# The opening of a fused attention layer: loads issued by three engines, forget columns loaded apart, squares shared, and the small weights cast on GpSimd

## The chip, the cores and the metric

The kernel runs on one core of a Trainium2 chip, as one launch. The metric is the device time of a launch in microseconds (us), lower is better. A core has five engines, each with its own in-order instruction queue: TensorE (PE in the profile, its weight loads PEld), VectorE (DVE), ScalarE (ACT), GpSimd (POOL) and SyncE (SP). 16 DMA engines serve them all.

## The reference

One layer over 512 rows of x behind 16 learned meta rows (L = 528), width 1024, all in float32:

```python
u = rmsnorm(h, pre_norm_g)
proj = u @ w_in
(cq, ckv, k_pe_raw, z_mla, fq, fk, fv, f_logit, z_fox, gate_a, gate_b) = split(proj)
q  = rmsnorm(cq, g_q) @ w_uq;  kv = rmsnorm(ckv, g_kv) @ w_ukv
y_mla = (attention(q, kv, rope(k_pe_raw)) * silu(z_mla)) @ w_br_mla
cum = cumsum(log_sigmoid(f_logit + fox_forget_b))
y_fox = (attention(fq, fk, fv, cum) * silu(z_fox)) @ w_br_fox
out = h + rmsnorm((sigmoid(gate_a) * y_mla + sigmoid(gate_b) * y_fox) @ w_out, g_post)
```

The opening, which the change touches, computes u and the four narrow pieces of proj: cq (256 columns of w_in), ckv (128), k_pe_raw (32), which lie side by side, and f_logit (16 columns, "forget columns"), which lie far off at column 4512.

## The kernel before

Each float32 product is made of three TensorE products in a narrower format: an operand is split into a high half (h) and a low half (l), and h*h, l*h and h*l are summed in PSUM. Splitting takes a cast (the high half) and a subtraction (the low half), and these are what ScalarE, VectorE and GpSimd do for most of the kernel.

The opening works on five blocks of rows: t = 0 to 3 are 128 rows of x each, t = 4 is the 16 meta rows. For each block:

- `load_h(t)` loads it into `ht`; block 0 comes as two halves of 512 columns, both issued by SyncE.
- `squares(t)` sums the squares of each row on ScalarE (tile `hn` takes the squares, `st` the sums), then square root and reciprocal. For block 0 the halves are two ScalarE instructions.
- `scaled(t)` multiplies the rows on VectorE (tile `hn`).
- `turn(t)` transposes it on TensorE in eight pieces of 128x128, into `pt`.
- `turned(t, 0, ..)` writes the high half of u transposed, `uTh`, on ScalarE, and `turned(t, 1, ..)` the low half, `uTl`, on VectorE, eight instructions each. `turned_all(4)` does it for the meta rows.
- `small(t, which, ks)` multiplies it with the narrow weights, into the PSUM tile `psm`: per k (eight pieces of 128 rows of the weights) the products 0 (uTh, wsh), 1 (uTl, wsh) and 2 (uTh, wsl).
- `back(t)` and `latent(t)` normalise the results (`sm`) and transpose them (`pc`).

The narrow weights, 432 columns, come in four quarters c (two k each), raw in `wsr`: for every quarter one load of 416 columns (128 partitions x 2 x 1664 B) and one of the 16 forget columns (128 x 2 x 64 B). `small_hi(c)` casts quarter c into `wsh`: quarters 0, 2 and 3 on ScalarE, quarter 1 on GpSimd. `small_lo(c)` subtracts into `wsl`: quarters 0 and 1 on GpSimd, 2 and 3 on VectorE. `spun` is a product whose result nobody reads: ten of them (512 columns) run on TensorE while the first loads are under way, and four more behind `turn(0)`. `wsplit` (wh, wl) splits all later weights in the same way, wh on ScalarE and wl on GpSimd.

The order in which the code calls these sets the order of TensorE's queue (`manual_schedule`). On the other engines a planner orders the instructions, but those wrapped in `pin` (`keep_in_program_order`) stay in the order of the code; `free` leaves the planner a choice. SyncE's loads share eight semaphores in turn, so a ninth load is issued once the first has landed.

Ahead of all this VectorE clears CT and ONE, and GpSimd makes the identity matrix `ident` for the transposes and clears KPL and `fa`. Behind it come the first projections (fq, fk, ppe, v) and 16 attention stages, then the branch products, gates and the output.

## Time and profile before

| | |
|---|---|
| three runs | 604.13, 604.9, 605.65 us, median 604.9 |
| profiled execution | 603.71 us, its span 601.8 us (1.9 us around it) |
| TensorE busy | 592.5 us, 98% of the span |
| VectorE, ScalarE, GpSimd busy | 374.1, 343.9, 180.6 us |
| granted TensorE clock | 0.998 |
| DMA moved | 93.25 MB, 155 GB/s on average |

The span runs from the first to the last instruction of the program. A row of the timeline has the start, the length, the engine, the line, the operation, the tiles out<-in and their shapes, and in brackets how long the engine sat idle before it and who ended that. "DMA a<-b" is a transfer. Rows of several instructions carry their count (x8), and their length is that of the whole group. Line numbers are those of the kernel before.

### The profile page before, as it was taken

How to read it: one execution, taken by the hardware profiler on the slowest of the kernel's cores; microseconds unless marked ns; L12 is line 12 of the kernel's file. 1: busy time of each engine (PE TensorE's matmuls, PEld its weight loads, DVE VectorE, ACT ScalarE, POOL GpSimd, SP SyncE). 2: the span in 40 equal slices, each digit the busy share in tenths (PEclk: the TensorE clock that was granted, in tenths of full speed). 3: DMA queues.
4: the chain of work that ended last, by engine and by line, in shares of the span. 5: the costliest groups of instructions: out<-in, count | busy, mean ns of one | idle time of the engine just before them, and what ended most of it. 6: DMA issues, size and time to landing. Idle time of an engine off the chain costs nothing.

```text
span 601.8 us, 10999 instructions
## 1 busy us (share of the span) xinstructions
PE 592.5 (98%) x3777; PEld 501.7 (83%) x3777; DVE 374.1 (62%) x1002; ACT 343.9 (57%) x788; POOL 180.6 (30%) x239
## 2 busy tenths in 40 slices
PE   8999999999999999999999999999999999999996
PEld 6889779789889889888898898888888888888884
DVE  4956776674675674766657747764733524367857
ACT  7847765774783784766747747851222423353653
POOL 4316635443348453443523534430000000000000
PEclk9999999999999999999999999999999999999999
DMA  8433699899796798988886875988533333332603
GB/s 294 107 84 86 134 196 208 193 189 231 96 185 152 171 200 178 189 191 170 163 158 154 201 160 140 193 163 281 182 97 105 106 86 89 105 104 91 228 0 141
DMA packets 219960, 93.25 MB, mean 155 GB/s; under 512 B 133420, under 2 KB 211636, under 8 KB 219904
## 3 DMA queue, kind: packets, MB, share of 16 engines
q1 hardware_dynamic: 219904, 92.55, 65.5%
q8 instruction: 30, 0.49, 0.3%
q14 instruction: 26, 0.21, 0.1%
HBM read 58.10 MB, written 4.00 MB: 103 GB/s over the span
## 4 chain that ended last, share of the span: by engine, by line
PE 92%; ACT 3%; DMA 2%; DVE 1%; issue 1%; POOL 1%; SPq 0%; DVEq 0%; ACTq 0%; POOLq 0%
PE z L97 16%; PE py L97 14%; PE pg L97 14%; PE v L97 9%; PE st L97 8%; PE fq L97 8%; PE fk L97 7%; PE ov L97 5%; PE x L97 4%; PE psm L97 2%; PE mq L97 2%; PE mk L97 1%; PE ppe L97 1%; DMA wsr<-in_w_in_dram 1%; PE y L97 1%; DMA ht<-in_x_dram 1%
## 5 line engine op out<-in xcount | busy, mean ns | idle before, releaser
L103 POOL TENSOR_TENSOR wl<-wraw,wh 128x1024 fp32r<-128x1024 f32 (+2 forms) x63 | 122.6, 1954 | 105.3 <-ACT wh L130 76.5
L130 ACT CAST wh<-wraw 128x1024 fp32r<-128x1024 f32 (+1 forms) x80 | 83.1, 1042 | 115.7 <-PE pg L97 38.6
L823 DVE SCALAR_TENSOR_TENSOR pn<-sf,ri,pn 128x128 f16<-128x128 f32 (+3 forms) x128 | 70.7, 592 | 13.9 <-ACT pn L822 13.8
L795 ACT ACTIVATE sf<-sf,nb 128x144 f32<-128x144 f32 (+3 forms) x128 | 72.0, 564 | 8.1 <-DVE nb L787 7.8
L822 ACT ACTIVATE pn<-sf,ri 128x128 f16<-128x128 f32 (+3 forms) x128 | 61.5, 551 | 20.4 <-ACT sf L795 17.6
L103 DVE TENSOR_TENSOR wl<-wraw,wh 128x1024 fp32r<-128x1024 f32 x33 | 40.3, 1223 | 42.4 <-ACT wh L130 42.4
L787 DVE CUSTOM_DVE_ANT_0 sf<-st,maskt 128x272 f32<-128x272 f32 (+2 forms) x128 | 48.6, 435 | 3.9 <-PE st L97 3.9
L97 PE MATMUL z<-uTh,wh 128*128 128x512 f32 x128 | 50.9, 398 | 0.0
L97 PE MATMUL z<-uTh,wl 128*128 128x512 f32 x128 | 50.1, 392 | 0.3 <-POOL wl L103 0.3
L97 PE MATMUL pg<-uTh,wh 128*128 128x512 f32 x128 | 50.3, 393 | 0.0
L97 PE MATMUL z<-uTl,wh 128*128 128x512 f32 x128 | 50.0, 391 | 0.0
L97 PE MATMUL pg<-uTl,wh 128*128 128x512 f32 x128 | 49.8, 389 | 0.0
L97 PE MATMUL pg<-uTh,wl 128*128 128x512 f32 x128 | 49.8, 389 | 0.0
L97 PE MATMUL py<-gh,wh 128*128 128x512 f32 x128 | 49.8, 389 | 0.0
L97 PE MATMUL py<-gl,wh 128*128 128x512 f32 x128 | 49.8, 389 | 0.0
L97 PE MATMUL py<-gh,wl 128*128 128x512 f32 x128 | 49.8, 389 | 0.0
L97 PE MATMUL st<-hlk,hlq 64*128 64x272 f32 (+3 forms) x480 | 47.3, 306 | 0.0
L97 PEld LDWEIGHTS st<-hlk,hlq 64*128 64x128 f32 x480 | 35.0, 185 | 5.8 <-ACT vh L719 2.8
L700 DVE TENSOR_REDUCE vsc<-v 128x1 f32<-128x272 f32 (+1 forms) x32 | 13.2, 432 | 37.9 <-PE v L97 37.9
L97 PE MATMUL v<-uTh,wl 128*128 128x256 f32 (+1 forms) x128 | 36.5, 285 | 0.0
L97 PE MATMUL fk<-uTl,wh 128*128 128x256 f32 (+1 forms) x128 | 36.4, 285 | 0.0
L97 PE MATMUL fk<-uTh,wh 128*128 128x256 f32 (+1 forms) x128 | 36.4, 285 | 0.0
(233 smaller groups left out, 1431.4 us busy)
## 6 DMA issues: line engine op xcount, KB each, us to landing
wraw<-in_w_in_dram SPq DMA_DIRECT2D x56, 512.0 KB, 4.1
wraw<-in_w_br_fox_dram SPq DMA_DIRECT2D x8, 512.0 KB, 3.6
tb<-in_w_out_dram SPq DMA_DIRECT2D x8, 512.0 KB, 7.4
wraw<-in_w_br_mla_dram SPq DMA_DIRECT2D x8, 512.0 KB, 3.6
wraw<-in_w_out_dram SPq DMA_DIRECT2D x6, 512.0 KB
pt<-pn SPq DMA_TRANSPOSE x128, 3.1
xr<-in_x_dram SPq DMA_DIRECT2D x4, 512.0 KB, 7.4
out_dram<-yo SPq DMA_DIRECT2D x8, 256.0 KB, 2.0
```

Of the source, the lines that this page charges most:

```text
L97: nc.tensor.matmul(*a, **k)
L103: return eng.tensor_tensor(out=lo, in0=src, in1=f32(hi), op=ALU.subtract)
L130: nc.scalar.copy(wh[:, :n], raw[:, :n])
L700: nc.vector.tensor_reduce(out=sc[:, i : i + 1], in_=ps, op=ALU.max, axis=AX.X, apply_absolute_value=True)
L787: nc.vector.tensor_tensor_reduce(out=sf_of(h, b)[:, c0 : c0 + w], in0=ps[h][:, o : o + w], in1=maskt[:, m0 : m0 + w], scale=-scale, scalar ...
L795: exps[g] = nc.scalar.activation(sf, sf, AF.Exp, bias=sums["nb"][:, h, b : b + 1], scale=-1.0, accum_out=sums["su"][:, h, b : b + 1]).ins
L822: nc.scalar.activation(hi, sf, AF.Copy, scale=rib)
L823: nc.vector.scalar_tensor_tensor(out=lo, in0=sf, scalar=rib, in1=hi, op0=ALU.mult, op1=ALU.subtract)
```

## The change

Six edits, all in the opening:

1. The second half of block 0 is issued by ScalarE, ahead of its table load and its first square root (`warm`), which now follow it.
2. The forget columns of all four quarters come in one load of their own (tile `wf`, 128 x 8 x 64 B), issued by GpSimd; `wsr` keeps 416 columns. GpSimd clears KPL behind that.
3. Block 0's second half is squared on VectorE (`tensor_tensor_reduce`), the first on ScalarE.
4. GpSimd casts the forget columns and all four quarters; it subtracts the forget columns, then quarters 0 and 1 as before.
5. TensorE runs the products of k = 0, 1 of block 0 ahead of `turn(1)`.
6. Eight and three `spun` instead of ten and four.

```diff
--- before.py
+++ after.py
@@ -234,7 +234,6 @@
     nc.vector.memset(f32(ONE), 0.0)
     for h in range(2):
         nc.vector.memset(f32(ONE[64 * h : 64 * h + 2, :]), 1.0)
-    nc.gpsimd.memset(f32(KP[1]), 0.0)
     hls = {}
 
     def hl_done(key, n, w):
@@ -276,7 +275,7 @@
         ppt = ph.enter_context(tc.tile_pool(name="ppt", bufs=2, space=PSUM))
         pps = ph.enter_context(tc.tile_pool(name="pps", bufs=2, space=PSUM, side="right"))
         warm = pa1.tile([1, 16], F32, tag="warm", name="warm")
-        nc.scalar.activation(warm[:, 0:1], eps_t[0:1, 0:1], AF.Sqrt)
+        pin = tc.keep_in_program_order
 
         hts = {}
         halves = (slice(0, 512), slice(512, D))
@@ -286,14 +285,18 @@
             pool, tag = (wp, "wraw") if t < 3 else (pa, "ht")
             hts[t] = pool.tile([128, D], F32, tag=tag, name=f"ht{t}")
             if t == 0:
-                for sl in halves:
-                    nc.sync.dma_start(hts[t][:, sl], x2[0:128, sl])
+                nc.sync.dma_start(hts[t][:, halves[0]], x2[0:128, halves[0]])
+                pin(nc.scalar.dma_start(hts[t][:, halves[1]], x2[0:128, halves[1]]))
             elif t < 4:
                 nc.sync.dma_start(hts[t], x2[128 * t : 128 * t + 128])
             else:
                 nc.sync.dma_start(hts[t][0:META], meta_tokens)
 
         load_h(0)
+        pin(nc.scalar.activation(warm[:, 0:1], eps_t[0:1, 0:1], AF.Sqrt))
+        wf = pa1.tile([128, KD, NH], F32, tag="wf", name="wf")
+        nc.gpsimd.dma_start(wf, win[:, :, O_F : O_F + NH])
+        nc.gpsimd.memset(f32(KP[1]), 0.0)
 
         g8 = pa1.tile([KD, 128], F32, tag="g8", name="g8")
         nc.sync.dma_start(g8, pre_norm_g[0].rearrange("(k p) -> k p", p=128))
@@ -304,17 +307,16 @@
         wsr = []
         nsm0 = NSM - NH
         for c in range(4):
-            r = pa.tile([128, 2, NSM], F32, tag="wsr", name=f"wsr{c}", bufs=4)
-            nc.sync.dma_start(r[:, :, 0:nsm0], win[:, 2 * c : 2 * c + 2, 0:nsm0])
-            nc.sync.dma_start(r[:, :, nsm0:], win[:, 2 * c : 2 * c + 2, O_F : O_F + NH])
+            r = pa.tile([128, 2, nsm0], F32, tag="wsr", name=f"wsr{c}", bufs=4)
+            nc.sync.dma_start(r, win[:, 2 * c : 2 * c + 2, 0:nsm0])
             wsr.append(r)
 
         def small_hi(c, copy):
-            return copy(wsh[:, 2 * c : 2 * c + 2, :], wsr[c])
+            return copy(wsh[:, 2 * c : 2 * c + 2, 0:nsm0], wsr[c])
 
         def small_lo(c, eng):
             cs = slice(2 * c, 2 * c + 2)
-            return eng.tensor_tensor(out=wsl[:, cs, :], in0=wsr[c], in1=f32(wsh[:, cs, :]), op=ALU.subtract)
+            return eng.tensor_tensor(out=wsl[:, cs, 0:nsm0], in0=wsr[c], in1=f32(wsh[:, cs, 0:nsm0]), op=ALU.subtract)
         for t in (2, 4, 3):
             load_h(t)
         gq = pa1.tile([128, R_Q + R_KV], F32, tag="gq", name="gq")
@@ -342,8 +344,9 @@
             st1 = sts[t] = pa.tile([128, 16], F32, tag="st1", name=f"st1_{t}")
             if t == 0:
 
-                for i, sl in enumerate(halves):
-                    pin(nc.scalar.activation(hn[:, sl], ht[:, sl], AF.Square, accum_out=st1[:, 2 + i : 3 + i]))
+                pin(nc.scalar.activation(hn[:, halves[0]], ht[:, halves[0]], AF.Square, accum_out=st1[:, 2:3]))
+                pin(nc.vector.tensor_tensor_reduce(out=hn[:, halves[1]], in0=ht[:, halves[1]], in1=ht[:, halves[1]], scale=1.0,
+                                                   scalar=0.0, op0=ALU.mult, op1=ALU.add, accum_out=st1[:, 3:4]))
                 pin(nc.vector.tensor_scalar(out=st1[:, 0:1], in0=st1[:, 2:3], scalar1=1.0 / D, scalar2=EPS, op0=ALU.mult,
                                             op1=ALU.add))
                 pin(nc.scalar.activation(st1[:, 1:2], st1[:, 3:4], AF.Sqrt, bias=st1[:, 0:1], scale=1.0 / D))
@@ -450,10 +453,9 @@
 
         order = tc.manual_schedule(engines={mybir.EngineType.PE})
         ph.enter_context(order)
-        pin = tc.keep_in_program_order
         free = lambda ins: ins
         spun = acc("spun")
-        for _ in range(10):
+        for _ in range(8):
             mm(spun, ONE, CT[:, 0:512], start=True, stop=True)
         gps = ppt.tile([128, 4, 128], F32, tag="pt", name="gps")
         tps(gps[:, 0, 0:KD], g8, ident[0:KD, 0:KD])
@@ -461,22 +463,23 @@
         scaled(0, pin)
         pin(nc.vector.tensor_copy(gcol, gps[:, 0, 0:KD]))
         turn(0)
-        for _ in range(4):
+        for _ in range(3):
             mm(spun, ONE, CT[:, 0:512], start=True, stop=True)
         squares(1, pin)
         scaled(1, pin)
-        pin(small_hi(0, nc.scalar.copy))
-        turn(1)
-        pin(small_hi(1, nc.gpsimd.tensor_copy))
+        pin(nc.gpsimd.tensor_copy(wsh[:, :, nsm0:], wf))
+        for c in range(4):
+            pin(small_hi(c, nc.gpsimd.tensor_copy))
         turned(0, 0, range(KD), pin)
         turned(0, 1, range(KD), pin)
-        for c in (2, 3):
-            pin(small_hi(c, nc.scalar.copy))
+        small(0, (0, 1), range(2))
+        turn(1)
+        pin(nc.gpsimd.tensor_tensor(out=wsl[:, :, nsm0:], in0=wf, in1=f32(wsh[:, :, nsm0:]), op=ALU.subtract))
         for c in (0, 1):
             pin(small_lo(c, nc.gpsimd))
         turned(1, 0, range(KD), pin)
         turned(1, 1, range(KD), pin)
-        small(0, (0, 1))
+        small(0, (0, 1), range(2, KD))
         small(1, (0, 1))
         for c in (2, 3):
             pin(small_lo(c, nc.vector))
```

On TensorE, from the first transposes on (pt out of hn are transposes of a block, psm are products with the narrow weights), before:

```order
L100 MATMUL pt_1_190<-ident,hn_175 128x128 x4
L97 MATMUL spun<-CT,ONE 128x512 x4
L100 MATMUL pt_0_206<-ident,hn_199 128x128 x4
L100 MATMUL pt_1_211<-ident,hn_199 128x128 x4
L97 MATMUL psm_253<-wsh,uTh 128x432
L97 MATMUL psm_253<-wsh,uTl 128x432
```

and of the change:

```order
L100 MATMUL pt_1_186<-ident,hn_171 128x128 x4
L97 MATMUL spun<-CT,ONE 128x512 x3
L97 MATMUL psm_221<-wsh,uTh 128x432
L97 MATMUL psm_221<-wsh,uTl 128x432
L97 MATMUL psm_221<-wsh,uTh 128x432
L97 MATMUL psm_221<-wsh,uTl 128x432
L100 MATMUL pt_0_226<-ident,hn_194 128x128 x4
L100 MATMUL pt_1_231<-ident,hn_194 128x128 x4
L97 MATMUL psm_221<-wsh,uTh 128x432
```

Four products of block 0 moved ahead of the transposes of block 1 (hn_199 before, hn_194 now). The rest of TensorE's queue is the same.

On GpSimd, from its first use of the narrow weights to the subtraction of the first later weights (wl), before:

```order
L328 MEMSET fa 16x528
L313 COPY wsh<-wsr_135 128x864
L317 TENSOR_TENSOR wsl<-wsr_132,wsh 128x864
L317 TENSOR_TENSOR wsl<-wsr_135,wsh 128x864
L103 TENSOR_TENSOR wl_582<-wraw_579,wh_581 128x1024
```

and of the change, with its load:

```order
L298 DMA wf<-in_w_in_dram 128x8x16
masks.py:199 ISA
masks.py:199 AFFINE_SELECT ident<-ident 128x128
L299 MEMSET KPL 128x528
L330 MEMSET fa 16x528
L470 COPY wsh<-wf 128x8x16
L315 COPY wsh<-wsr_134 128x2x416
L315 COPY wsh<-wsr_136 128x2x416
L315 COPY wsh<-wsr_138 128x2x416
L315 COPY wsh<-wsr_140 128x2x416
L477 TENSOR_TENSOR wsl<-wf,wsh 128x8x16
L319 TENSOR_TENSOR wsl<-wsr_134,wsh 128x2x416
```

One cast became five, and they stand ahead of the two subtractions; ScalarE has none of them any more.

On VectorE, between the subtractions of quarters 2 and 3 and the results of block 0 (st_2, st_4, st_3 and hn are the scaling of blocks 2, 4 and 3; um and uTl<-um the meta rows; tm and sm belong to back(0)), before:

```order
L317 TENSOR_TENSOR wsl<-wsr_141,wsh 128x864
L333 RECIPROCAL st_2_290<-st_2_290 128x1
L358 TENSOR_SCALAR hn_289<-ht_144,st_2_290 128x1024
L333 RECIPROCAL st_4_296<-st_4_296 16x1
L358 TENSOR_SCALAR hn_295<-ht_146,st_4_296 16x1024
L390 TENSOR_TENSOR um_0_358<-pt_0_340,gcol 128x64
L390 TENSOR_TENSOR um_1_362<-pt_1_345,gcol 128x64
L423 TENSOR_TENSOR tm_319<-psm_253,rt 128x16
L333 RECIPROCAL st_3_302<-st_3_302 128x1
```

and of the change:

```order
L319 TENSOR_TENSOR wsl<-wsr_140,wsh 128x2x416
L335 RECIPROCAL st_2_287<-st_2_287 128x1
L361 TENSOR_SCALAR hn_286<-ht_142,st_2_287 128x1024
L335 RECIPROCAL st_4_293<-st_4_293 16x1
L361 TENSOR_SCALAR hn_292<-ht_144,st_4_293 16x1024
L335 RECIPROCAL st_3_299<-st_3_299 128x1
L361 TENSOR_SCALAR hn_298<-ht_146,st_3_299 128x1024
L426 TENSOR_TENSOR tm_316<-psm_221,rt 128x16 x4
L335 RECIPROCAL st_0_313<-st_0_313 128x2
L393 TENSOR_TENSOR um_0_355<-pt_0_337,gcol 128x64
L428 TENSOR_TENSOR sm_312<-tm_316 128x32
```

The planner put the scaling of block 3 and most of back(0) ahead of the meta rows. On ScalarE the square of block 3 stands ahead of the first square of back(0) now, not behind it.

## The prediction

> **What bounds the kernel now.** I read the shares by engine first, then the chain that ended last over the first 62 us, then the timeline of each engine over the first 34 us.
>
> ```profile
> PE 592.5 (98%) x3777; PEld 501.7 (83%) x3777; DVE 374.1 (62%) x1002; ACT 343.9 (57%) x788; POOL 180.6 (30%) x239
> ```
>
> TensorE (PE) is busy for 98% of the span, so only a stage in which it waits can give time back. The chain of waits, whose columns are start, length and what held the end, shows where that is:
>
> ```profile
> 2.05 4.12 DMA ht<-in_x_dram
> 6.19 5.47 DMA wsr<-in_w_in_dram
> ...
> 11.74 0.92 ACT wsh L313
> ...
> 13.72 0.36 DVE uTl L379
> ...
> 14.13 4.82 PE psm L97 x23
> ...
> 19.44 1.04 ACT hn L352 x2
> ...
> 29.07 0.63 PE pc L100 x4
> 29.70 4.76 PE psm L97 x24
> ```
>
> Up to 14.13 us the end hangs on the second row block of x, on the small weights (wsr), on ScalarE's cast of their last quarter and on the first split of row block 1. After 14.13 PE runs almost without a break, and from 29.07 the chain stays with it. So the change is worth what it moves at one place: the start of the transposes of latent(1), 29.07 us. All the code that it moves lies ahead of that.
>
> **The loads.** SyncE (SP) issues all loads; its timeline:
>
> ```profile
> 0.72 0.87 SPq L290 DMA_DIRECT2D ht<-in_x_dram  x2
> 7.24 0.34 SPq L292 DMA_DIRECT2D ht<-in_x_dram  x1
> 11.51 0.33 SPq L326 DMA_DIRECT2D fb<-in_fox_forget_b_dram  x1
> ```
>
> One of the two L290 issues goes to ScalarE, so the second row block, issued at 2.05, goes out 0.45 us earlier. The last column but one below is the busy share of the DMA engines:
>
> ```profile
> 3.50:4.00 0.50, 0.50 (x3) 0.39 (x2) 0.00 (x0) 0.50 (x2) 0.00 (x0) 1.00 0.63 168
> 4.00:4.50 0.50, 0.50 (x3) 0.40 (x2) 0.15 (x1) 0.46 (x3) 0.00 (x0) 1.00 0.83 298
> ```
>
> They idle for (0.37 + 0.17) x 0.5 = 0.27 us there because the queue was filled too slowly. That gap closes, and the four forget loads (L309, 16 KB each) no longer stand between the quarters, but the same 64 KB now passes the same engines from another queue. Bounds: the quarters land no earlier than before, or 1.1 us earlier (the gap and four places of 0.2). I take 0.4, nearest to the measured gap: ht1 at 5.8 (was 6.17), quarter 0 at 6.9 (SP's L292 at 7.24 waited for it) and quarter 3 at 11.1 (L326 at 11.51 waited for it). The block 0 halves then land together: ScalarE squares one, VectorE the other.
>
> ```profile
> 4.14 0.63 ACT L346 ACTIVATE hn<-ht 128x512 f32<-128x512 f32 x1
> 6.49 1.09 PE L100 MATMUL pt<-ident,hn 128*128 128x128 f32 x8
> L787 DVE CUSTOM_DVE_ANT_0 sf<-st,maskt 128x400 f32<-128x400 f32 x6 | 3.2, 570 | 0.0
> ```
>
> ScalarE loses a square of 0.63. The new VectorE reduction isn't in this trace; its nearest row, the same instruction on 400 columns, took 570 ns, so about 0.7 for 512 (bounds 0.6 and 0.9). Block 0 was transposed at 7.58 with the squares one after the other; side by side it is some 0.6 sooner, 7.0, and not needed before ScalarE is free for it at 7.2 (below). So neither bound costs anything.
>
> **The first splits.** Now the engines' own rows:
>
> ```profile
> 7.38 0.30 ACT L332 ACTIVATE st<-st,eps_t 128x1 f32<-128x1 f32 x1
> 7.58 0.90 ACT L313 CAST wsh<-wsr 128x864 fp32r<-128x864 f32 x1
> 8.38 2.16 ACT L382 ACTIVATE uTh<-pt,gcol 128x128 fp32r<-128x128 f32 x8
> 9.35 0.90 POOL L313 CAST wsh<-wsr 128x864 fp32r<-128x864 f32 x1 [7.09 <-DMA wsr<-in_w_in_dram]
> 9.55 2.16 DVE L379 SCALAR_TENSOR_TENSOR uTl<-pt,gcol,uTh 128x128 fp32r<-128x128 f32 x8 [0.88 <-ACT uTh L382]
> 10.22 4.07 POOL L317 TENSOR_TENSOR wsl<-wsr,wsh 128x864 fp32r<-128x864 f32 x2
> 12.56 2.17 ACT L382 ACTIVATE uTh<-pt,gcol 128x128 fp32r<-128x128 f32 x8
> 13.72 2.16 DVE L379 SCALAR_TENSOR_TENSOR uTl<-pt,gcol,uTh 128x128 fp32r<-128x128 f32 x8 [2.02 <-ACT uTh L382]
> 15.80 2.02 DVE L317 TENSOR_TENSOR wsl<-wsr,wsh 128x864 fp32r<-128x864 f32 x2
> 17.19 1.75 PE L97 MATMUL psm<-wsl,uTh 128*128 128x432 f32 x8
> 17.93 0.75 DVE L358 TENSOR_SCALAR hn<-ht,st 128x1024 f32<-128x1024 f32 x1
> ```
>
> ScalarE loses three casts of 0.9. uTh(0) starts behind L332, at 7.2 instead of 8.38. VectorE's uTl(0) starts when four uTh are done (9.55 against 8.38 here), so at 8.4. GpSimd has quarter 0 cast at 6.9 + 0.9 = 7.8. PE's four early matmuls end at 9.3, the transposes of block 1 follow, and their first half is there at 9.9. So uTh(1) runs 9.9 to 12.05 (was 12.56) and uTl(1) 11.1 to 13.25 (was 13.72 to 15.88): 2.6 us earlier.
>
> GpSimd's last cast ends at 11.1 + 0.9 = 12.0, where PE takes up quarter 3 (ScalarE's ended at 12.66). From there 4 + 16 matmuls at 0.198 (4.76 for 24) end at 15.9. The low-weight matmuls of psm0, at 17.19 in the row, could start then: 1.2 us gained so far.
>
> **Where it is lost again.** GpSimd has four casts now and only then its subtractions: the forget columns (128 of 864 columns, 0.3), then quarter 0 at 12.3 to 14.3 and quarter 1 to 16.25 (2.04 x 832/864 each). VectorE wants to subtract quarters 2 and 3 at 13.25, while before GpSimd was done (14.29) when VectorE began (15.80). What happens when both want two operands in SBUF:
>
> ```profile
> 25.16 6.00 POOL L103 TENSOR_TENSOR wl<-wraw,wh 128x1024 fp32r<-128x1024 f32 x3 [10.87 <-ACT wh L130]
> 46.06 2.41 POOL L103 TENSOR_TENSOR wl<-wraw,wh 128x1024 fp32r<-128x1024 f32 x1
> 52.93 5.24 POOL L103 TENSOR_TENSOR wl<-wraw,wh 128x1024 fp32r<-128x1024 f32 x2 [4.47 <-ACT wh L130]
> 25.69 1.92 DVE L425 TENSOR_TENSOR sm<-tm 128x32 f32<-128x32 f32 x1
> 33.33 0.19 DVE L425 TENSOR_TENSOR sm<-tm 128x32 f32<-128x32 f32 x1
> 53.49 2.42 DVE L533 SCALAR_TENSOR_TENSOR ch<-fa,ch 16x528 fp32r<-16x528 f32 x1
> ```
>
> The 32-column L425 takes 0.19 with GpSimd idle, and 1.92 when it starts 0.53 into a GpSimd subtraction of 2.41: it ends at 27.6, with that instruction. L533 ends 0.56 behind GpSimd's first of two (55.35), and the pair takes 5.24 instead of 4.82. So one waits for the other's whole instruction, and they take turns. By turns here: VectorE's quarter 2 waits from 13.25 to 14.3 and ends at 15.25; GpSimd's quarter 1 runs to 17.2; VectorE's quarter 3 to 18.2. PE ends psm0 at 18.6 (17.19 + 1.75 = 18.94 before); the scaling of block 2, behind quarter 3 on VectorE, ends at 19.05, and PE's transposes of block 2 start at 19.1.
>
> ```profile
> 18.77 1.66 PE L100 MATMUL pt<-ident,hn 128*128 128x128 f32 x16
> 24.96 0.60 PE L100 MATMUL pc<-ident,sm 128*128 128x128 f32 x4
> PE pc L100 <- ACT uTh L382: 0.3, 1, 0.3
> ```
>
> That is 0.33 late against 18.77. VectorE's new order puts the scaling of block 3 and back(0) ahead of the meta rows, on which psm4 waits, so PE doesn't catch all of it up; of 0 to 0.33 I take 0.2 at latent(0): 25.15 for 24.96. But the square of block 3 (L352, 1.04 in the chain) moves into the time in which ScalarE waits for psm0, so what follows psm0 on ScalarE, and GpSimd's weight subtractions that wait for it, come 0.7 to 0.9 earlier, and the 0.3 that PE waits ahead of latent(1) goes: from 25.15 the transposes (4 + 8, 1.3 from the rows 24.96 and 6.49 with their gaps) and 12 matmuls (2.4) lead to 28.85, against 29.07. **Sum: -0.2 us.** The profiled execution took 603.71 us (span 601.8 and 1.9 around it), which becomes 603.5; the median of the three runs is 604.9, so I predict 604.7. With quarter 3 landing 0.8 earlier than I take, the same walk gives -1.0; with no load earlier, +0.6.
>
> The Trainium skill speaks against this change in "SBUF — State Buffer", section "Who interferes with whom": a VectorE instruction with two SBUF inputs and a GpSimd instruction that reads SBUF exclude each other for the whole instruction. L425 and L533 bear that out. It also counts copies and tensor_scalar in the doubled mode, which no row here shows against GpSimd; by it the scaling of block 1 waits 0.2 us for quarter 0's cast, which would change the sum by nothing, as uTl(0) starts at 8.4 in any case.
>
> **The rivals.**
>
> *The subtractions don't get in each other's way where it counts.* Then VectorE's are done at 15.2, GpSimd's quarter 1 at 16.25, psm0 ends at 17.6 and block 2 follows at once: 1.3 us gained at psm0, 1.6 at latent(1), 603.3; with loads 0.8 earlier 2.2, 602.7. For it: uTl(0) at 9.55, with one operand in PSUM, kept its 2.16 beside GpSimd. Against it: L425 and L533.
>
> *Slower: the forget columns come late over GpSimd's queue.* They are the first thing that GpSimd casts, and every small matmul reads them. No transfer from that queue is in this trace. The nearest row is a forget load on SP:
>
> ```profile
> DMA to landing us min/median/max: 5.5/5.5/5.5
> ```
>
> Issued at 1.0, that lands at 6.5, ahead of quarter 0, and costs nothing. At the other end, four in a row as now (2.92 to 11.66) give 9.7. It decides from 8.5 on: from there GpSimd's four casts end later than quarter 3's landing lets them, and each us costs one. At 9.7 that is +1.2, 606.1. A descriptor generation that held GpSimd past 5.5 us would keep back the identity matrix too, for PE's first transposes.
>
> *Slower: PE's clock stays low.* The filler matmuls warm it:
>
> ```profile
> 2.07 4.34 PE L97 MATMUL spun<-CT,ONE 128*128 128x512 f32 x10 [2.07 <-DVE ONE L236]
> 7.34 1.18 PE L97 MATMUL spun<-CT,ONE 128*128 128x512 f32 x4
> ```
>
> Ten took 434 ns each, the later four 295. Eight end at 5.5 and leave 0.1 to 0.5 us idle. If PE ran psm0 and psm1 at the pace of the ten (0.36 for 432 columns instead of 0.198), its 20 matmuls from 12.0 on would end 3.3 later, at 19.2, and the eight low ones at 20.8 to 22.1, 1.9 to 3.2 behind the 18.94 of now: 606.8 to 608.1. In "TensorE: Matmul & The Clock Gate" the Trainium skill (section "Part 1: The HAM clock gate") has the clock rise after one busy window of some 3.4 us, of free phase. By it eight matmuls are just enough or just not; the ten here were enough.
>
> **How the numbers follow.** Forecast 0.57, no mutual wait 0.22, late forget columns 0.10, low clock 0.06, and 0.05 for what shifts later, in the attention stages. A measurement of this kernel can tell about 0.3%, 1.8 us, from no change. Faster by more than that: half of the first rival (0.11), 0.06 of the forecast with early loads, 0.03 of the rest, 0.20. Slower by more: the low clock (0.06), 0.04 of the late columns, 0.02 each of forecast and rest, 0.14. Within: 0.66. The range takes in the first rival's 602.7 and the late columns' 606.1, and 0.3 below and 0.8 above them for the spread of the runs (604.13 to 605.65): 602.4 to 606.9.
>
> **What would show it.** uTh(1) near 10 and uTl(1) near 11; GpSimd's quarter 3 cast at 11 to 12; VectorE's two subtractions of wsl at 13 to 18, one or both of 2 us or more instead of 1.05; block 2's transposes at 19.1; latent(1)'s at 28.9. If those subtractions take 1.05 each, the first rival holds. If GpSimd's cast of wf starts behind 8.5, the second; if psm matmuls behind 12 us are 0.36 apart, the third. Loads that land over 0.8 us from what I take would make the sum wrong without touching its mechanism.

## The result, and the profile after

The changed kernel is slower: median of 22 runs 606.2 us (605.0 to 608.91) against 604.15 us (603.17 to 605.65, 22 runs) on the same chip, ratio 1.0035 with a 95% interval of 1.0025 to 1.0045, so +2.05 us. The time lies in the range on record (602.4 to 606.9), but the forecast was 0.2 us less than before, next to no change, and that doesn't hold.

The profiled execution took 608.46 us, span 606.6. Its shares say nothing of the cause, since PE, the engine that sets the end, is as busy as before:

```profile
PE 591.8 (98%) x3774; PEld 501.7 (83%) x3774; DVE 376.2 (62%) x1004; ACT 341.4 (56%) x783; POOL 185.9 (31%) x245
```

Its chain of waits over the first 62 us (start, length, what held the end) answers to the chain of before:

```profile
1.33 7.78 DMA wf<-in_w_in_dram
...
9.16 0.83 POOL wsh L470
...
10.87 1.06 PE psm L97 x4
...
16.76 2.81 DVE wsl L319
...
20.47 1.15 ACT hn L355 x2
...
31.41 0.44 PE pc L100 x4
31.85 4.73 PE psm L97 x24
```

Before, the last quarter of the weights and ScalarE's cast of it led to TensorE at 14.13. Now the forget columns (wf) do, then GpSimd's casts, VectorE's second subtraction with 2.81 us in place of 1.05, and the square of block 3 (L355). The transposes of latent(1) start at 31.25 in the timeline instead of 29.07, 2.2 us late (their row has 0.60 us from there, of which the chain counts the last 0.44).

One execution is not the kernel, though. The landings of the loads differ between executions, so both kernels were profiled again, unchanged: before twice (before_2, before_3), after three times (after_again, after_3, after_4). The table has the times in us at which ScalarE starts on block 1, quarter 3 of the weights has landed, the transposes of block 2, of latent(0) and of latent(1) start, the first attention product (fq) starts, and the span:

| run | block 1 | quarter 3 | block 2 | latent(0) | latent(1) | fq | span | span behind fq |
|---|---|---|---|---|---|---|---|---|
| before | 6.20 | 11.66 | 18.77 | 24.96 | 29.07 | 37.38 | 601.8 | 564.4 |
| before_2 | 7.29 | 12.29 | 19.41 | 25.59 | 29.71 | 38.02 | 602.3 | 564.3 |
| before_3 | 5.77 | 11.82 | 18.95 | 25.14 | 29.24 | 37.55 | 602.3 | 564.8 |
| after | 7.38 | 12.64 | 20.49 | 27.57 | 31.25 | 39.50 | 606.6 | 567.1 |
| after_again | 6.16 | 11.21 | 19.09 | 26.16 | 29.83 | 38.09 | 604.1 | 566.0 |
| after_3 | 6.98 | 11.55 | 19.39 | 26.47 | 30.15 | 38.41 | 606.0 | 567.6 |
| after_4 | 6.38 | 11.33 | 19.17 | 26.25 | 29.93 | 38.18 | 604.8 | 566.6 |

By the medians of the columns fq comes 0.75 us late (38.30 against 37.55), and what lies behind fq takes 2.4 us more (566.85 against 564.4), although the change touches nothing there. That is more than the 2.05 us of the timed runs (profiled executions scatter by a us and more), but its division stands: **the smaller part arises in the opening, the larger one behind it.** The chain of after_4, whose loads landed early, is the better picture of the opening:

```profile
1.59 4.76 DMA ht<-in_x_dram
...
8.09 1.39 DVE hn L361
...
15.45 2.80 DVE wsl L319
...
19.15 1.15 ACT hn L355 x2
...
30.09 0.44 PE pc L100 x4
```

The forget columns are off the chain here. VectorE's scaling of block 1, its second subtraction and the square of block 3 stay on it.

What TensorE waited for in the whole execution, first in before, then in after, then in after_4 (us in total, times, longest). The psm row belongs to the opening, the ov rows to the part behind fq:

```profile
PE ov L97 <- DMA pt<-pn: 0.3, 1, 0.3
```

```profile
PE psm L97 <- POOL wsh L315: 2.8, 1, 2.8
PE ov L97 <- DMA pt<-pn: 2.1, 3, 0.9
```

```profile
PE ov L97 <- DMA pt<-pn: 1.9, 2, 1.4
```

In the attention stages pn are the normalised attention weights; a DMA transposes them (pt<-pn), and ov are their products with the values. So the products ov wait for these transposes: a wait whose code the change doesn't touch, and which is longer with it. It is 2.1, 1.6, 2.7 and 1.9 us in the four executions of after, 0.3, none and 0.5 in the three of before.

### The profile page after: what moved, and what is told of

Read it like the earlier page. It is cut to its first block, busy times and chain, and to the rows that moved or that the text cites. A ratio compares the mean times of both kernels' runs of the same rounds, so it can differ in the third digit from the quotient of the medians.

```text
span 606.6 us, 10990 instructions
## 1 busy us (share of the span) xinstructions
PE 591.8 (98%) x3774; PEld 501.7 (83%) x3774; DVE 376.2 (62%) x1004; ACT 341.4 (56%) x783; POOL 185.9 (31%) x245
## 4 chain that ended last, share of the span: by engine, by line
PE 91%; DVE 2%; DMA 2%; ACT 2%; POOL 1%; issue 1%; DVEq 0%; POOLq 0%; ACTq 0%
PE z L97 15%; PE py L97 14%; PE pg L97 14%; PE v L97 9%; PE st L97 8%; PE fk L97 8%; PE fq L97 7%; PE ov L97 5%; PE x L97 4%; PE psm L97 2%; PE mq L97 2%; DMA wf<-in_w_in_dram 1%; DMA pt<-pn 1%; PE mk L97 1%; PE ppe L97 1%; PE y L97 1%
```

## The experiments

Theories at the start: that the late forget columns set the time (L in the expectations), or the turns that VectorE and GpSimd take at the weight subtractions (X). Later came the scatter of the landings (S), that the second loss is a matter of when TensorE reaches the attention stages, whatever made it late (P), and SyncE's queue as its place (Q). The expectations name two more: K, that lateness is only carried on and the second loss belongs to the changed code; and, in those of the repeats alone, Q stands for something else, that loads over three queues are late more often. Where nothing else is said, a ratio is that to the kernel before on the same chip, with its 95% interval.

### a1_wf_on_sp: forget columns by SyncE's queue, behind block 1

```
-        nc.gpsimd.dma_start(wf, win[:, :, O_F : O_F + NH])
...
         load_h(1)
+        nc.sync.dma_start(wf, win[:, :, O_F : O_F + NH])
```

> The changed kernel, but the forget columns (wf) are issued by SyncE right behind the second row block instead of by GpSimd. Theory L (the late forget columns set the time, as the second rival had it): GpSimd's first cast starts near 7 instead of 9.16 us, block 1's transposes at 10.6 instead of 11.9, everything behind follows, latent(1) near 30.1 instead of 31.41, and the time falls by 1.2 us, to 605.0. Theory X (the turns that VectorE and GpSimd take in their subtractions, behind a late last quarter, set it): GpSimd's fourth cast still starts with the landing of quarter 3, near 12.6, its subtractions near 13.5, VectorE's second subtraction still ends near 19.5, latent(1) stays between 31.2 and 31.4, and the time stays within 0.3 us of 606.2, except for what quarter 3 lands earlier.

606.91 us, 1.0038 [1.0020, 1.0056]. GpSimd's timeline shows that the columns came in time:

```profile
6.88 0.29 POOL L470 CAST wsh<-wf 128x128 fp32r<-128x128 f32 x1 [4.62 <-DMA wf<-in_w_in_dram]
```

Cast by 7.2, ahead of quarter 0 (8.13), and nothing gained. L falls as the cause of the median. VectorE's two subtractions took 1.26 and 2.81, the transposes of block 2 followed at 19.28: X held.

### a2_no_gp_sub: GpSimd without its two subtractions

The low halves of quarters 0 and 1 are set to zero and their subtraction is left out.

```
+        nc.gpsimd.memset(f32(wsl[:, 0:4, 0 : NSM - NH]), 0.0)
...
-        for c in (0, 1):
-            pin(small_lo(c, nc.gpsimd))
```

> The changed kernel without GpSimd's subtractions of quarters 0 and 1: their low halves are cleared early instead, so the products with them add nothing. Theory X (turns between VectorE and GpSimd): VectorE's two subtractions take 1.05 us each and end at 17.8 instead of 19.57, block 2 is scaled at 18.7 instead of 20.4, its transposes follow the products of block 0 at 19.8, latent(1) comes at 29.7 to 30.1 instead of 31.41, and the time falls by 1.3 to 1.7 us, to 604.5 to 604.9. Theory L (late forget columns): VectorE's subtractions are not what the end waits for, block 2 moves by less than 0.3 us and the time stays at 606.2 within 0.4.

604.87 us, 0.9999 [0.9983, 1.0015]: the loss of the changed kernel is gone. VectorE's subtractions took 1.02 each. The edit also spares GpSimd 4.7 us, so what it does later comes sooner, and this run alone can't tell that from the turns; a3 below keeps the two subtractions. The times of the profiled execution can't be compared with the others, because TensorE's clock was low in it (length, PE busy, granted clock, DMA share, GB/s by stretch):

```profile
11.00:12.00 1.00, 1.00 (x4) 0.71 1.16 388
12.00:13.00 1.00, 1.00 (x6) 0.50 0.98 295
13.00:14.00 1.00, 1.00 (x6) 0.50 0.99 351
```

Its fq is at 39.54 for that reason.

### b1_x_half_act and b2_wf_gpsimd: two parts of the change alone

In the kernel before, the second half of block 0 issued by ScalarE; and, apart from that, the forget columns as wf over GpSimd's queue, cast and subtracted there.

```
-                for sl in halves:
-                    nc.sync.dma_start(hts[t][:, sl], x2[0:128, sl])
+                nc.sync.dma_start(hts[t][:, halves[0]], x2[0:128, halves[0]])
+                pin(nc.scalar.dma_start(hts[t][:, halves[1]], x2[0:128, halves[1]]))
```

```
+        wf = pa1.tile([128, KD, NH], F32, tag="wf", name="wf")
+        nc.gpsimd.dma_start(wf, win[:, :, O_F : O_F + NH])
...
-            nc.sync.dma_start(r[:, :, nsm0:], win[:, 2 * c : 2 * c + 2, O_F : O_F + NH])
...
+        pin(nc.gpsimd.tensor_copy(wsh[:, :, nsm0:], wf))
```

> The kernel before, but the second half of row block 0 is issued by ScalarE ahead of its table load. If the second issuing queue is what made block 1 late: block 1 (6.17 before) lands past 6.9 and quarter 3 (11.66 before) past 12.2, and the time rises by 0.5 to 1.0 us. If it is innocent, as the prediction had it: block 1 lands at 5.7 to 6.2, quarter 3 at 11.2 to 11.7, and the time is 603.7 to 604.2.

> The kernel before, but the forget columns come in one load over GpSimd's queue, are cast and subtracted on GpSimd apart, and the quarters have 416 columns; casts and all else as before. If GpSimd's queue is what made the loads late: wf lands near 9.1, block 1 lands past 6.9 and quarter 3 past 12.2, ScalarE's cast of quarter 3 and uTh(1) shift by 0.6 to 1.0, and the time rises by 0.6 to 1.0 us to 604.8 to 605.1. If it isn't: block 1 lands at 6.2 or before, quarter 3 at 11.5 or before, and the time is 604.15 within 0.3, although wf itself may land at 9.

b1: 605.52 us, 1.0006 [0.9989, 1.0023]; b2: 605.72 us, 1.0015 [0.9994, 1.0036]. Neither part gains anything, and neither alone is shown to lose. In their profiles block 1 was ready at 7.41 and 7.78 and fq started at 38.4 in both. That is a little later than in any of the three profiles of before (7.29 and 38.02 at most, below), so a small cost of either part isn't excluded.

### after_again, after_3, after_4, before_2, before_3: both kernels unchanged

> The changed kernel once more, unchanged, for a second profile beside the others on one chip. If its late landings (block 1 at 7.35, quarter 3 at 12.64, wf at 9.11) belong to the kernel, they come again within 0.3 us; if they are the scatter of one execution, some of them come up to 1.2 us earlier, as they did when SyncE issued wf. TensorE's granted clock may fall to 0.5 for some 3.4 us from 11 us on, as it did once: then its products end 1.6 us later. Time against the kernel before: 1.0035 within 0.0017.

> The changed kernel, unchanged, a third profile. It has shown fq at 39.50 with wf at 9.11 and quarter 3 at 12.64, and at 38.09 with wf at 7.88 and quarter 3 at 11.21. Theory Q: in these two further executions wf lands at 7 to 9 and quarter 3 past 12.2 at least once. Both theories: with quarter 3 at 11.2 to 11.7 and wf under 8.5 fq starts at 38.0 to 38.3, with quarter 3 at 12.6 at 39.5, since VectorE and GpSimd take turns in either case.

> The changed kernel, unchanged, a fourth profile; the same expectations as for the third. If fq is at 38.1 in both, the openings of the two kernels differ by 0.7 us in most executions and not by 2.1, and the rest of the 2.0 us of the medians has to be looked for behind fq.

> The kernel before, unchanged, for a second profile of its loads. Theory Q (the loads over three queues are late more often): block 1 lands within 0.3 us of 6.17, quarter 3 within 0.4 of 11.66, and the first product of fq starts within 0.4 of 37.38. Theory S (each execution draws its landings anew, whichever queue they use): some landing of the kernel before is 1 us later, too, and fq with it.

> The kernel before, unchanged, a third profile; the same expectations as for the second: fq at 37.4 within 0.4 by theory Q, up to 1.2 later in one of the two by theory S.

after_again: 606.44 us, 1.0032 [1.0016, 1.0048]; the other four, one run each: after_3 607.74 and after_4 606.63, before_2 604.03 and before_3 604.16. Their times are in the table above. Block 1 is ready at 5.8 to 7.3 before and at 6.2 to 7.4 after, quarter 3 at 11.7 to 12.3 and at 11.2 to 12.6: the same load scatters by 0.6 to 1.5 us in either kernel, and in the repeats of after none came as late as in its first profile. S holds. wf landed at 9.1, 7.9, 7.1 and 7.1.

### a5_square3_later: square of block 3 behind back(0) again

```
         scaled(4, pin)
+        small(0, (2,))
+        sms = {0: back(0)}
         squares(3, pin)
         scaled(3, pin)
-        small(0, (2,))
-        sms = {0: back(0)}
```

> The changed kernel with block 3's square and scaling called behind back(0), so that ScalarE takes up psm0 (21.53 in the changed kernel) without first waiting for block 2's scaling and squaring block 3. If that order costs something: ScalarE squares psm0 within 0.2 us of its end instead of 1.2 us behind it, the meta rows' low half comes 0.9 us nearer to block 2's transposes, latent(1) comes 0.5 to 0.9 earlier relative to block 2's transposes, and the ratio to the kernel before falls from 1.0035 to 1.0020 to 1.0027. If it is hidden, as the prediction had it (the square fills a wait), latent(1) keeps its distance of 10.9 us from block 2's transposes (20.49 to 31.41) and the ratio stays at 1.0035.

606.18 us, 1.0038 [1.0019, 1.0056]. ScalarE's timeline shows the intended order:

```profile
19.41 0.38 ACT L421 ACTIVATE sm<-psm 128x256 f32<-128x256 f32 x1 [2.90 <-PE psm L97]
...
21.27 1.08 ACT L355 ACTIVATE hn<-ht 128x1024 f32<-128x1024 f32 x1
```

latent(0) came 5.95 us behind block 2's transposes instead of 7.07 to 7.08, latent(1) 10.15 instead of 10.74 to 10.76: the moved square costs 0.6 us at latent(1) in the trace. The time doesn't show it: the ratio is no lower than that of the changed kernel, where 1.0020 to 1.0027 was expected. In this execution block 1 was ready at 7.33, and fq started at 38.04.

### a6_more_spun: fourteen filler products instead of three behind block 0

```
-        for _ in range(3):
+        for _ in range(14):
             mm(spun, ONE, CT[:, 0:512], start=True, stop=True)
```

> The changed kernel with 14 filler products behind block 0's transposes instead of 3, which fill TensorE's idle time from 8.0 to 10.87. If the low clock (the third rival: 0.50 granted from 11.3 to 14.6 in one execution, none in two others) is part of the median: the clock stays at 1.00, the highest times go from some 608.5 to 607 and the ratio falls from 1.0035 to 1.0020 to 1.0028. If it is not: ratio 1.0035 within 0.0008, no product of psm is more than 0.1 us later, and only the clock column differs in some executions.

607.14 us, 1.0040 [1.0022, 1.0057]. The clock was 1.00 throughout, and nothing was gained. That doesn't clear the clock by itself, because the fillers cost time: GpSimd had cast quarter 0 by 9.54, and they kept the first product back to 11.07, 1.5 us. What speaks against the clock is that its mean over the execution has the median 0.998 in the 22 timed runs of the changed kernel, and 0.998 also in the runs of the kernel before that accompany a1 and a2 (0.001 of it is 0.6 us).

### a3_casts_scalar: quarters 2 and 3 cast on ScalarE again

```
-        for c in range(4):
+        for c in (0, 1):
             pin(small_hi(c, nc.gpsimd.tensor_copy))
...
+        for c in (2, 3):
+            pin(small_hi(c, nc.scalar.copy))
```

> The changed kernel with quarters 2 and 3 cast on ScalarE behind uTh(0), as before; GpSimd casts the forget columns and quarters 0 and 1. Theory X (turns between the subtractions): GpSimd starts to subtract at 10.0 to 11.5 instead of 12.1 to 13.6 and is done by 15.5, VectorE's two subtractions take 1.0 each, no turn is taken, block 2's transposes come at 18.2 to 18.9 with early loads instead of 19.1 to 19.4, and fq 0.3 to 0.8 earlier than the 38.1 to 38.4 of the changed kernel. If the turns cost nothing, uTh(1), which waits for quarter 3's cast again, makes it as late as before or later: fq at 38.1 or more.

605.63 us, 1.0014 [0.9998, 1.0030]. The subtractions of the weights (line L319; ns of one as minimum, median, maximum), first in after_4, then here:

```profile
L319 POOL TENSOR_TENSOR wsl<-wsr,wsh x2: 1992/2380/2767, 12.7 to 14.6; 128x832 fp32r<-128x832 f32 x2
...
L319 DVE TENSOR_TENSOR wsl<-wsr,wsh x2: 1159/1981/2803, 14.4 to 15.5; 128x832 fp32r<-128x832 f32 x2
```

```profile
L319 POOL TENSOR_TENSOR wsl<-wsr,wsh x2: 1977/1979/1981, 11.0 to 12.9; 128x832 fp32r<-128x832 f32 x2
L319 DVE TENSOR_TENSOR wsl<-wsr,wsh x2: 1015/1018/1020, 15.9 to 16.8; 128x832 fp32r<-128x832 f32 x2
```

GpSimd is done at 14.9, before VectorE begins, and the turns are gone: block 2 at 18.83, fq at 37.74, 0.56 earlier than the changed kernel's median, and by the ratios (1.0035 and 1.0014, whose intervals overlap a little) 1.3 us of time less. X held again.

### best2: an opening that gains

In the kernel before, GpSimd casts quarters 0 and 1, ScalarE casts 2 and 3 behind uTh(1), TensorE takes the products of both blocks in turns of k, and the square of block 3 stands behind the first one of back(0).

```
+        for c in (0, 1):
+            pin(small_hi(c, nc.gpsimd.tensor_copy))
         turn(1)
...
+        for ks in (range(4), range(4, 6), range(6, KD)):
+            small(0, (0, 1), ks)
+            small(1, (0, 1), ks)
```

> The kernel before with its loads as they were, but: GpSimd casts quarters 0 and 1, ScalarE casts 2 and 3 behind uTh(1) instead of ahead of it, TensorE takes the products of blocks 0 and 1 in turns (k 0 to 3 of both, then 4 and 5, then 6 and 7), and block 3's square is pinned where it stood. Theory X (what counts is when both subtractions of VectorE are done without meeting GpSimd's, and when block 2's transposes start): uTh(1) runs at 9.9 to 12.1, GpSimd subtracts from 10 to 14, VectorE from 14 to 16.1, block 2 is scaled at 17, psm0 ends at 17.1, block 2's transposes start at 17.2 instead of 18.77, latent(1) at 27.5 instead of 29.07, and the ratio to the kernel before is 0.9973 (602.5 for 604.15). Against it: quarters that land 1.0 late shift all of this by 1.0 but the kernel before as well; if only the loads set the time, the ratio is 1.000 within 0.001.

604.61 us, 1.0001 [0.9987, 1.0015]. Block 2's transposes at 18.08 (17.2 expected), fq at 36.66: 0.7 us ahead of the kernel before. The span behind fq is 567.5 instead of 564.3 to 564.8. So in this profile a gain in the opening is given back, as a loss is enlarged, and the time shows no gain.

### d0_one_spun_less and d1_delay: a delay and nothing else

d0 has one filler product less in the kernel before (a control); d1 has ten more transposes ahead of latent(1).

```
-        for _ in range(10):
+        for _ in range(9):
             mm(spun, ONE, CT[:, 0:512], start=True, stop=True)
```

```
+            for _ in range(10 if t == 1 else 0):
+                tps(pc[:, 0, :rows], sm[:rows, 0:128], ident[:rows, :rows])
```

> A control: the kernel before with nine filler products instead of ten, one TensorE instruction less and nothing else. No theory has it change the opening: fq starts at 37.4 to 38.1 as in three profiles of the kernel before, the stretch from the first fq to the end takes 564.3 to 564.8, and the ratio is 1.000 within 0.001. If that stretch takes 565.5 or more, merely another program of nearly the same text (its place in memory, its instruction fetches) has the loss behind fq, and no phase and no wait of the change explains it.

> The kernel before with ten more transposes of the same block into the same place ahead of latent(1): TensorE comes 1.0 to 1.1 us later to fq, nothing else is changed. Theory P (SyncE's queue of transposes meets another phase and costs another 1 us at the ov products of 106.6): fq at 38.4 to 39.1, the ov products 1.8 to 2.3 later than 106.60, ratio 1.003 to 1.004. Theory K (a lateness that comes from TensorE is carried or swallowed, and the second loss belongs to the changed code): the ov products 0.3 to 1.1 later, the stretch behind fq at 564.3 to 565, ratio 1.0005 to 1.0018.

d0: 605.13 us, 1.0002 [0.9987, 1.0016]; fq 37.80, 564.9 behind it. d1: 606.42 us, 1.0027 [1.0007, 1.0047]; fq 38.52, 1.14 us later than in the profile of before, 567.4 behind it. TensorE at the place where the delays stop being equal, in before, before_2, after_4 and d1:

```profile
106.60 0.40 PE L97 MATMUL ov<-pt,vp 80*64 80x512 f16 x1
107.30 2.01 PE L97 MATMUL ov<-pt,vp 80*64 80x512 f16 x25 [0.30 <-DMA pt<-pn]
109.24 0.65 PE L97 MATMUL st<-hlk,hlq 64*128 64x272 f32 x6
```

```profile
107.28 2.05 PE L97 MATMUL ov<-pt,vp 80*64 80x512 f16 x26
109.26 0.64 PE L97 MATMUL st<-hlk,hlq 64*128 64x272 f32 x6
```

```profile
107.17 0.36 PE L97 MATMUL st<-CT,ONE 64*128 64x400 f32 x2
108.91 0.38 PE L97 MATMUL ov<-pt,vp 80*64 80x512 f16 x1 [1.38 <-DMA pt<-pn]
109.80 2.01 PE L97 MATMUL ov<-pt,vp 80*64 80x512 f16 x25 [0.51 <-DMA pt<-pn]
```

```profile
108.78 0.38 PE L97 MATMUL ov<-pt,vp 80*64 80x512 f16 x1 [0.81 <-PE st L97]
109.75 2.01 PE L97 MATMUL ov<-pt,vp 80*64 80x512 f16 x25 [0.59 <-DMA pt<-pn]
```

In before_2, 0.64 us late at fq, TensorE doesn't wait and is only 0.02 late behind these products. In after_4, 0.80 late at fq, it waits 1.9 us and is 2.50 late at the 25 products; in d1, 1.14 late at fq, 2.45. SyncE issues the transposes that they wait for; its queue in before, before_2, after_4 and d1, start and length of the issues:

```profile
95.95 0.53 SPq L91 DMA_DIRECT2D QP<-qpe_dram  x1
96.57 4.54 SPq L91 DMA_TRANSPOSE pt<-pn  x3
...
101.84 3.41 SPq L91 DMA_TRANSPOSE pt<-pn  x2
```

```profile
101.91 3.35 SPq L91 DMA_TRANSPOSE pt<-pn  x2
```

```profile
97.34 1.98 SPq L91 DMA_DIRECT2D QP<-qpe_dram  x1
99.41 3.89 SPq L91 DMA_TRANSPOSE pt<-pn  x3
...
104.03 3.64 SPq L91 DMA_TRANSPOSE pt<-pn  x2
```

```profile
104.16 3.52 SPq L91 DMA_TRANSPOSE pt<-pn  x2
```

The last two transposes leave 0.07 us later than before in before_2, 2.19 later in after_4 and 2.32 later in d1. Their inputs aren't what they wait for: VectorE has written the last pn at 97.5, 98.2, 98.3 and 98.8, over 3 us before these issues. So a delay with nothing of the change in it gives the same loss at these products: the trace shows P for a delay of 1.1 us. The time agrees, but its interval (0.4 to 2.8 us) doesn't tell 1.1 us from more. The control says that another program text alone doesn't give the loss.

The other profiles bear this out, f1 and f2 aside, which move loads there. I compare the start of the same product with its start in before, at 106 us and at these ov products. In eleven profiles (the four of after, a1, a2, a3, a6, b1, b2, d1) TensorE is 0.74 to 2.18 us late at 106, and every one loses another 0.9 to 1.7 at the products. In the other six (before_2, before_3, d0, a5, d2, best2) it is at most 0.69 late, or early, and they go from a gain of 0.7 to a loss of 0.8. So it is lateness that goes with the larger loss, in old and new code alike; but it isn't lateness at fq alone, since a3 is only 0.36 late at fq and 0.82 at 106.

### d2_best_delay: the same for best2

best2 with seven such transposes:

```
+            for _ in range(7 if t == 1 else 0):
+                tps(pc[:, 0, :rows], sm[:rows, 0:128], ident[:rows, :rows])
```

> The kernel of the best2 run with seven more transposes of the same kind ahead of latent(1), 0.7 to 0.8 us, which gives fq back the start of the kernel before, near 37.4. Theory P (phase): the stretch behind fq takes 564.3 to 565 again, as in the kernel before, and the ratio stays at 1.000 or falls under it. Theory K: that stretch keeps its 567.5 and the ratio rises from 1.0001 by the delay to 1.0012 to 1.0025.

605.17 us, 1.0011 [0.9995, 1.0028]; fq 37.78, 566.4 behind it. Taken whole, this fits neither expectation: the opening of before restored in time, to 0.4 us, doesn't bring back the 564.4 behind it. By place, d2 loses only 0.35 at the ov products of 107 us, as P has it, and 1.65 at 256 to 260 us, where the control loses 1.2 too.

### f1_delay_relief and f2_best_relief: later weight loads taken off SyncE's queue

d1 and best2, with the loads of raw weights 10 to 16 issued by GpSimd:

```
-            dma(rv, src)
+            dma(rv, src, nc.gpsimd.dma_start if 10 <= u <= 16 else None)
```

> The kernel of the delay run (ten more transposes ahead of latent(1)), with the weight loads of the first attention stages (wraw 10 to 16, between 80 and 106 us) issued by GpSimd instead of SyncE, eight issues of some 0.5 us each that SyncE is spared. Theory Q (SyncE's serial queue of issues makes the transposes late at the ov products of 106.6): SyncE is there 2 us or more sooner, the ov products are 1.1 to 1.4 us later than 106.60, as the delay alone makes them, instead of 2.2 to 2.4, and the ratio falls from 1.0027 to 1.0010 to 1.0020. If the transposes are late for what they wait for or for the DMA engines' traffic, the ov products stay 2 us or more late. GpSimd loses some 1.1 us for each issue, which can make its subtractions late; that would show as a wait of the projections for wl ahead of 106.

> The kernel of the best2 run with the same loads issued by GpSimd. Theory Q: the 0.7 us that its opening gains are kept at the ov products of 106.6 (0.5 to 0.9 us earlier than 106.60, where they were 0.17 earlier and 0.12 later in the best2 run), and the ratio falls from 1.0001 to 0.9980 to 0.9992, unless the second place at 256 us, which has no such relief, takes it back. If it isn't SyncE's issues: no change against best2, ratio 1.000, or more where GpSimd's issues delay its subtractions.

f1: 611.13 us, 1.0098 [1.0069, 1.0128]; f2: 609.39 us, 1.0078 [1.0052, 1.0104]. The relief made a stall of its own; what the products z, a projection, waited for in f1:

```profile
PE z L97 <- POOL wl L103: 4.2, 1, 4.2
```

GpSimd's first such load stood in its queue ahead of the subtraction of wl and waited about 3 us for its buffer. TensorE then reached ov so late that the transposes were there. Q is neither shown nor refuted by these two.

## Why the prediction failed, point by point

**The loads (0.4 us earlier).** Failed as a gain, at little cost. Quarter 3 landed at 11.2 to 11.6 in three of four executions of after (predicted 11.1) and 11.7 to 12.3 before; block 1, issued 0.46 us earlier (1.59 for 2.05), was ready no earlier (6.2 to 7.4, predicted 5.8). The error was to take a landing of one execution for a property of the kernel.

**The first splits (uTh(1) at 9.9).** Failed: 11.12 in after_4, the row quoted next. TensorE's timeline there shows why, and VectorE's behind it:

```profile
8.99 0.46 PE L97 MATMUL psm<-wsh,uTh 128*128 128x432 f32 x1 [1.00 <-POOL wsh L315]
9.79 0.47 PE L97 MATMUL psm<-wsh,uTl 128*128 128x432 f32 x1 [0.34 <-DVE uTl L382]
...
10.48 1.03 PE L100 MATMUL pt<-ident,hn 128*128 128x128 f32 x8
```

```profile
8.09 1.39 DVE L361 TENSOR_SCALAR hn<-ht,st 128x1024 f32<-128x1024 f32 x1
...
14.37 3.88 DVE L319 TENSOR_TENSOR wsl<-wsr,wsh 128x832 fp32r<-128x832 f32 x2
```

```profile
11.12 2.18 ACT L385 ACTIVATE uTh<-pt,gcol 128x128 fp32r<-128x128 f32 x8 [1.20 <-PE pt L100]
```

The four products that were moved ahead of block 1's transposes wait for GpSimd's cast of quarter 0 (8.05 to 8.93 here), which I had ended at 7.8, and for a uTl that came a us later than my 8.4. And the scaling of block 1 took 1.39 where it takes 0.75 alone: it started 0.04 us behind that cast. In the profiled execution of after it was the other way round: the scaling came first, and GpSimd's cast of wf took 0.83 where it takes 0.29 alone. The prediction said that no row showed a one-input instruction waiting for GpSimd, and left it at nothing. The rows show it now, as the Trainium skill has it in "SBUF — State Buffer", section "Who interferes with whom": copies and tensor_scalar can hold the pair of ports that VectorE shares with GpSimd, and whoever comes second is blocked for the whole instruction. Here that is 0.6 us where I had 0.2.

It cost nothing at block 2, though. VectorE's first subtraction started at 14.37 instead of 13.25, but GpSimd's, for which it would have waited, ended at 14.65 (14.3 predicted). That this lateness fell into that wait is luck.

**The turns.** Right, in mechanism and size: 3.88 us for VectorE's two subtractions beside GpSimd, 1.95 to 2.04 without, and block 2's transposes at 19.09, 19.39 and 19.17 in three of four executions, 19.1 predicted (how close that came is in part the luck just named). a2 and a3 bear it out.

**The walk from block 2 to latent(1).** This step failed, with the wrong sign: "the square of block 3 (L352, 1.04 in the chain) moves into the time in which ScalarE waits for psm0, so what follows psm0 on ScalarE, and GpSimd's weight subtractions that wait for it, come 0.7 to 0.9 earlier". In after_4, ScalarE:

```profile
19.15 1.06 ACT L355 ACTIVATE hn<-ht 128x1024 f32<-128x1024 f32 x1 [3.13 <-DVE hn L361]
...
20.21 0.36 ACT L421 ACTIVATE sm<-psm 128x256 f32<-128x256 f32 x1
...
22.75 0.44 ACT L395 CAST uTh<-um 128x64 fp32r<-128x64 f32 x2
```

and TensorE's meta product:

```profile
23.10 0.35 PE L97 MATMUL psm<-wsh,uTh 128*128 128x176 f32 x1 [0.46 <-ACT uTh L395]
```

The square can't use the wait: it is released only by VectorE's scaling of block 2 (hn L361 in the row), and that stands behind VectorE's subtractions. By the kernel's text the reason is the tile st: its pool has two buffers, so block 3's sums go where block 2's lay, which that scaling reads. The square starts at 19.15, about when psm0 is ready, and keeps the squares of psm0 back to 20.21. The prediction's own times, 18.6 for the end of psm0 and 19.05 for that scaling, already left no wait for it. Behind them VectorE does the scaling of block 3 and back(0) and only then the meta rows (22.20), whose cast is the L395 row; TensorE's meta product psm4 waits 0.46 us for it. For that order I took 0.2 late at latent(0), "of 0 to 0.33". Measured: latent(0) 7.08 us behind block 2's transposes instead of 6.19, so 0.9 us lost, and 1.3 late (26.25 for 24.96); the 0.25 that TensorE waited ahead of latent(1) did go, as predicted. latent(1) came at 29.83 to 30.15 (31.25 in after) instead of 28.85. In the traces a5 gives 0.6 of it back.

Two further profiles tell the order from the turns. a3 has no turns and loses the same: its square starts at 18.70, the squares of psm0 at 19.76, latent(0) comes 6.96 behind block 2. In a2 the slow clock made psm0 late, and there the square does fit into the wait, as the prediction had it; latent(0) comes 6.26 behind:

```profile
19.22 1.06 ACT L356 ACTIVATE hn<-ht 128x1024 f32<-128x1024 f32 x1 [1.20 <-DVE hn L362]
...
21.55 0.38 ACT L422 ACTIVATE sm<-psm 128x256 f32<-128x256 f32 x1 [1.18 <-PE psm L97]
```

**The premise.** "So the change is worth what it moves at one place: the start of the transposes of latent(1), 29.07 us" failed too, and it is the larger term. It had a chance of 0.05 ("what shifts later, in the attention stages"). In the changed kernel the shift runs through unchanged to the ov products at 107 us and grows there to 2.0 to 3.1 us, because SyncE's queue of transposes is later still than TensorE. d1 shows in its trace that a delay alone does this. How much later the queue gets is not in proportion: 0.64 us at fq vanished (before_2), 0.80 became 2.5 (after_4), and the 0.7 of best2 was lost. What makes the queue late by more than the delay stays open. In after_4 it is 0.9 late at 80 us and 2.2 at 104, and the issue of QP took 1.98 instead of 0.53; in d1 it is 1.8 late at 80 us already, and QP took 0.53 as before. Further on, at 256 to 260 us, another 0.7 to 2.2 us are lost in most of the profiles. One of the kernel before (before_2, 0.8) and the control (1.2) are among them, and two of the four of after (after_again, after_4: 0.2 at most) are not, so that place is not told apart by the change.

**The rivals.** No mutual wait: false. Late forget columns, from 8.5 us on: it occurred (9.1 in after, where TensorE waited 2.8 us), in two of nine executions with the columns on GpSimd's queue, but a1 shows that it doesn't make the median. Low clock: in one profile (a2) of nine with the new opening, and the mean clock of the timed runs (at a6) is that of before.

## What to carry to other kernels

Profile a change in the first microseconds several times before reading it: here the landings moved by 1.5 us between executions of the same kernel, as much as the change was about. A gap on one engine can be filled only by work whose buffers and inputs are there in the gap. Ask that of each moved instruction, not only whether its engine is idle. And a shift is not worth its own size where a serial queue stands behind: find the first place where the busy engine meets another queue with little slack, and take its price as uncertain on both sides.

## What the runs showed of the hardware that I had not expected

- A small transfer from GpSimd's queue at the start is slow: issue to landing in the profile of after (KB each, median us to landing), beside 7.1 to 7.9 as the time at which it landed in the three repeats.

```profile
wf<-in_w_in_dram POOLq DMA_DIRECT2D x1, 64.0 KB, 7.8
```

  The Trainium skill's page "DMA: Bandwidth & Descriptors" has, in its section "Anatomy of one DMA — SWDGE (gpsimd) path", a fit of 2.0 us plus the bytes at 436 GB/s; by it these 64 KB would take an estimated 2.15 us. The trace doesn't agree: eight runs of 64 bytes on each of 128 partitions, beside the loads of x and of the weights from other queues, took 5.8 to 7.8.
- TensorE's granted clock fell to 0.50 for more than 2 us behind a wait of 2.06 us in a2, and stayed at 1.00 behind a longer wait of 2.8 us in after.
- VectorE's scaling of a 128x1024 tile and GpSimd's cast hold each other up: 1.39 for 0.75 (after_4), and 0.83 for 0.29 (after).
